# Attention's blocks re-paced over six projection slabs, the gate's operands formed inside the last slab, and a written TensorE order behind it

## The chip, the cores and the metric

The kernel runs on one core of a Trainium2 chip. The metric is the device time of one execution in microseconds (us). TensorE (PE) multiplies, VectorE (DVE), ScalarE (ACT) and GpSimd (POOL) work elementwise, and the queue of SyncE (SP) issues most loads.

## The reference

A trunk of two layers over 512 tokens of width 1024, in float32. Layer 0 is a causal convolution module, layer 1 differential attention with 8 heads; each is followed by a SwiGLU feed-forward part and a gated embedding of the layer's own input `p`. The change touches layer 1's attention, the projection of `p` for its gate, and the product with `w_o`. Cut to that:

```python
u = rms_norm(h, attn_norm_g)
q, k, v = split(u @ w_qkv, 3)             # q, k: 8 heads x 2 halves of 64; v: 8 heads of 128
q = rms_norm(q, q_g) * 64 ** -0.5         # per head and half
k = rms_norm(k, k_g)
for each of 4 blocks of 128 queries, each head, halves c = 0, 1:
    probs[c] = softmax(q[c] @ k[c].T + bias, causal)
    w = probs[0] - lam * probs[1]
    o = w @ v
h = h + (rms_norm(o, sub_g) * (1 - lambda_init)) @ w_o
...                                       # swiglu
h = h + sigmoid(rms_norm(h, ple_g) @ ple_w_gate) * (p @ ple_w_proj)
```

## The kernel before, in words

Every float32 product is done as three products of a reduced format (`mm3`): each operand is split into a high part and a low part. For weights, `weight` loads a 512 KB piece on SP's queue into the ring `wraw` of two buffers (L145), ScalarE casts the high part `whi` (L149), and VectorE, or POOL where `eng=G`, subtracts to get `wlo` (L151). `whi` and `wlo` have four buffers each. A ring buffer is free for the next load when the subtraction that reads it has ended.

The order of instructions on each engine is fixed ahead of time by a scheduler which simulates the program; it follows the order of the code, but lets later instructions go first where an engine would stand idle in its simulation. Each engine then runs its list strictly in that order.

Queries, keys and values are computed in six slabs, in the order of `QKV`: q0, v0, q1, q2, v1, q3. A q slab gives queries and keys of two heads, a v slab the values of four. A slab takes four `weight`s and runs over four blocks of 128 tokens (`tokens`: 8 x 3 products of 128x512 each). For a q slab, each token block ends in `unit` (ScalarE L757, L760; VectorE's sum L764; a root on POOL, L237; POOL's scaling L767) and, a token block later, in `unit_end`: four transposes on TensorE (L773), four evictions on ScalarE (L781, L782), two copies on POOL (L786), and four subtractions on VectorE (L789, L791).

Between a slab's products stand pieces of attention. There are 8 heads x 4 blocks; block (hd, qb) has 128 queries and 128 (qb + 1) keys, and three stages. S: for each half two score products (L818, L819), a biased maximum on VectorE (L821), the exponential on ScalarE (L825), then the weighted difference on VectorE (L828 to L830). T, two blocks later: transposes (L838), split on ScalarE and VectorE (L840, L841). A, three blocks later: products with the values (L854, L855), every second time their sum (L861, L862), and after a head's fourth block the sums for its norm (L866 to L876). `stages` holds all stages in order, each with its block's number n. `pace` tells how much is taken in each token block: 3 x `pace` stages.

Behind the slabs stands the code that the change rewrites. `pfeatures` splits the two operands of `p` (loads L273, ScalarE L274, L275 on VectorE here and on POOL in layer 0) into the tiles C0 and C1; `project` forms eight outputs m, each of six products, from two `weight`s, with a `step` (one stage; when a head is complete, also `stage_o`: transposes L883 and a split by L180 on ScalarE, L181 on VectorE into the A tiles) before each m and after each three products. Then `linear` multiplies with `w_o`: eight outputs of 24 products each; m = 0 and m = 1 run together over k, and the first head whose `ot` is not ready is stepped first.

Of the kernel before, what the change touches and what calls it, by code (L numbers as in the profile page):

```python
# [13 lines left out]
F32R = mybir.dt.float32r  # L14
AF = mybir.ActivationFunctionType
ALU = mybir.AluOpType
# [4 lines left out]
P = 128  # L21
S = 512
D = 1024
NC = D // P
NH = 8
# [49 lines left out]
LA = 3  # L75
# [1 line left out]
PACK = True  # L77
E1 = True
GLO = 1
QKV = (("q", 0, (0, 0, 0, 0)), ("v", 0, (0, 1, 1, 0)), ("q", 1, (1, 1, 2, 2)), ("q", 2, (0, 1, 2, 0)), ("v", 1, (1, 2, 2, 2)), ("q", 3, (0, 2, 0, 1)))  # L80


@with_exitstack
def trunk(ctx, tc, xT, pT, wts, diag, dww, vec, rel, onehot, lamv, out):
    nc = tc.nc
    V, A, G, T = nc.vector, nc.scalar, nc.gpsimd, nc.tensor
# [20 lines left out]
    f = lambda ap: ap.bitcast(F32)  # L107
# [16 lines left out]
    t = wk()[:, 0:P]  # L124
# [4 lines left out]
    t = tp()  # L129
# [4 lines left out]
    wnext = [0]  # L134
    loaded = [None]

    def weight(n=1024, pieces=1, between=(), eng=V, after=(None, None), home=None):
        i = wnext[0]
        wnext[0] += 1
        raw = sb([P, 1024], *(home or ("wraw", 2)))  # L140
        hi = sb([P, 1024], "whi", 4, F32R)
        lo = sb([P, 1024], "wlo", 4, F32R)
        for k in range(pieces):
            cut = slice(k * n // pieces, (k + 1) * n // pieces)
            loaded[0] = nc.sync.dma_start(raw[:, cut], wts[i, :, cut])  # L145
            if k < len(between):
                between[k]()
            with tc.issue_after(after[1].ins) if after[1] else nullcontext():
                A.copy(hi[:, cut], raw[:, cut])  # L149
            with tc.issue_after(after[0].ins) if after[0] else nullcontext():  # L150
                eng.tensor_tensor(lo[:, cut], raw[:, cut], f(hi[:, cut]), ALU.subtract)  # L151
        return hi, lo
# [10 lines left out]
    def both(t):  # L163
        return t[:, 0], t[:, 1]
# [105 lines left out]
    def pfeatures(layer, parts):  # L270
        for k, (hi, lo) in enumerate(parts):
            raw = sb([P, 1024], "wraw", 2)[:, :S]
            nc.sync.dma_start(raw, pT[layer, :, k * S : (k + 1) * S])  # L273
            A.copy(hi, raw)  # L274
            (G if layer == 0 else V).tensor_tensor(lo, raw, f(hi), ALU.subtract)  # L275
        return parts

    last_product = [None]
# [231 lines left out]
    pp = []  # L510
# [67 lines left out]
            if c == 3:  # L578
                third = lo, hi

    def linear(n_in, src, consume, group0=1, before=None, after=None, split={}, home=None):


        m = 0
        while m < NC:
            g = group0 if m == 0 else 1
            ws = [weight(n_in * P, after=split.get(m + i, (None, None)), home=home if m + i == 2 else None) for i in range(g)]
# [290 lines left out]
    ot = {}  # L878
# [15 lines left out]
            if 0 <= at < len(todo):  # L894
                stages.append((n, partial(stage, *todo[at])))

    def take(n):
        got, stages[:n] = [s for _, s in stages[:n]], []
        return got

    waiting = None
    for what, at, pace in QKV:
        ws = slab(GLO if at > 0 else 0)
        for tb in range(4):
            between = take(3 * pace[tb])
# [12 lines left out]

    def step():
        if stages:  # L920
            n, s = stages.pop(0)
            s()
        else:
            n = 99
        while done[0] < NH and (n - LA - 3) // 4 > done[0]:
            stage_o(done[0])
            done[0] += 1

    ph = pfeatures(1, [both(sb([P, 2, S], t, 2, F32R)) for t in ("C0", "C1")])
    pp = []  # L930
    for m in range(NC):
        if m % 4 == 0:
            w = weight()
        step()
        if m < 2:
            o = sb([P, S], f"D{m + 2}", 1)
        elif m % 2 == 0:
            o2 = sb([P, 2, S], f"C{m // 2 + 1}", 2)
            o = o2[:, 0]
        else:  # L940
# [148 lines left out]
```

## Time and profile before

| | |
|---|---|
| Median of 3 runs | 1295.92 us (1295.68 to 1297.31) |
| Profiled execution, time | 1293.82 us |
| Its span on the core | 1292.0 us |
| Mean granted TensorE clock | 0.995 |
| TensorE busy | 1269.5 us (98%) |
| VectorE, ScalarE, POOL busy | 736.9, 521.6, 236.8 us |
| Six slabs | about 640 to 785 us |
| Last of the slabs to the end of `w_o` | 785 to about 881 us |

The profile's page gives each engine's busy time over the span, 40 equal slices of the span, and groups of instructions by line. A row of the timeline has the start, the duration (the modelled end of a matmul overlaps the next), the engine, the line, the tile written and the tiles read, and in brackets the idle time before it with what ended it. A row of waits has the waiting engine and line, then what released it, the total, the number of times, and the longest.

### The profile page before, as it was taken

The numbers are of one execution on the slowest core, as the hardware profiler recorded it, in microseconds if no ns is written. First come the engines' busy times: TensorE is split into PE (matmuls) and PEld (weight loads), VectorE is DVE, ScalarE is ACT, GpSimd is POOL, SyncE is SP. The second block draws the span as 40 slices with busy tenths as digits, with TensorE's granted clock in tenths as the row PEclk, the third lists the DMA queues.
The fourth block names the chain that finished last, engine by engine and source line by source line (L and its number), as shares of the span: only waits on it lengthen the run. The fifth ranks groups of instructions, "written<-read, shape, count | busy, mean of one in ns | idle before, by whom it ended". The sixth has DMA issues, their size and how long they took to land.

```text
span 1292.0 us, 15534 instructions
## 1 busy us (share of the span) xinstructions
PE 1269.5 (98%) x5960; PEld 1053.6 (82%) x5960; DVE 736.9 (57%) x1143; ACT 521.6 (40%) x826; POOL 236.8 (18%) x199
## 2 busy tenths in 40 slices
PE   9999999999999999999999997989999999999998
PEld 8888788888888888888888886878888888888887
DVE  4897866543344334457678988845443344334445
ACT  5742554332222223345566766634222233222332
POOL 1753432000000000042526534121000000000020
PEclk9999999999999999999999998999999999999999
DMA  7555223333333322233222223123333333332231
GB/s 273 192 177 181 80 76 104 98 98 98 98 98 99 97 86 95 82 117 98 88 90 74 74 66 83 57 76 103 99 98 94 89 97 96 98 98 90 90 115 66
DMA packets 46839, 131.98 MB, mean 102 GB/s; under 512 B 5379, under 2 KB 9987, under 8 KB 46764
## 3 DMA queue, kind: packets, MB, share of 16 engines
q1 hardware_dynamic: 44640, 127.55, 31.0%
q10 hardware_dynamic: 2124, 3.43, 1.0%
q8 instruction: 47, 0.77, 0.2%
q14 instruction: 28, 0.23, 0.1%
HBM read 126.75 MB, written 4.21 MB: 101 GB/s over the span
## 4 chain that ended last, share of the span: by engine, by line
PE 88%; DVE 6%; DMA 3%; issue 2%; ACT 1%; POOL 0%; SPq 0%; DVEq 0%; POOLq 0%; ACTq 0%
PE mm L156 28%; PE mm L157 27%; PE mm L158 27%; DVE sc L419 2%; DVE wlo L151 1%; PE tp L173 1%; PE mm L854 1%; DMA wraw<-in_wts 1%; DMA po<-big 1%; PE sc L818 1%; PE sc L368 1%; PE sc L819 1%; PE tp L838 1%; PE tp L773 0%; DMA h<-in_xT 0%
## 5 line engine op out<-in xcount | busy, mean ns | idle before, releaser
L149 ACT CAST whi<-wraw 128x1024 fp32r<-128x1024 f32 (+2 forms) x213 | 217.6, 1026 | 554.6 <-PE mm L158 364.1
L156 PE MATMUL mm<-A,wlo 128*128 128x512 f32 (+1 forms) x1096 | 427.9, 390 | 4.5 <-DVE wlo L151 3.0
L157 PE MATMUL mm<-A,whi 128*128 128x512 f32 (+1 forms) x1096 | 425.7, 389 | 0.0
L158 PE MATMUL mm<-A,whi 128*128 128x512 f32 (+1 forms) x1096 | 421.8, 389 | 0.0
L151 DVE TENSOR_TENSOR wlo<-wraw,whi 128x1024 fp32r<-128x1024 f32 (+2 forms) x209 | 259.4, 1245 | 84.8 <-ACT whi L149 84.7
L156 PEld LDWEIGHTS mm<-A,wlo 128*128 128x128 f32 x1096 | 206.0, 188 | 48.5 <-DVE wlo L151 3.5
L157 PEld LDWEIGHTS mm<-A,whi 128*128 128x128 f32 x1096 | 206.0, 188 | 42.8 <-issue 1.2
L158 PEld LDWEIGHTS mm<-A,whi 128*128 128x128 f32 x1096 | 205.4, 188 | 42.3 <-issue 0.5
L204 POOL TENSOR_TENSOR acc<-acc,wk 128x512 f32<-128x512 f32 x35 | 58.2, 1662 | 772.3 <-issue 660.1
L156 PE MATMUL mm<-B,wlo 128*128 128x512 f32 x352 | 137.8, 391 | 0.0
L157 PE MATMUL mm<-B,whi 128*128 128x512 f32 x352 | 137.4, 390 | 0.0
L158 PE MATMUL mm<-B,whi 128*128 128x512 f32 x352 | 137.4, 390 | 0.0
L635 DVE TENSOR_TENSOR h<-mm,h 128x512 f32<-128x512 f32 x48 | 33.0, 691 | 122.6 <-PE mm L158 122.5
L627 DVE TENSOR_TENSOR big<-mm,rb 128x512 f32<-128x512 f32 x44 | 30.4, 691 | 126.4 <-PE mm L158 126.4
L625 DVE TENSOR_TENSOR big<-mm,rb 128x512 f32<-128x512 f32 x44 | 30.4, 691 | 99.8 <-PE mm L158 93.0
L158 PEld LDWEIGHTS mm<-B,whi 128*128 128x128 f32 x352 | 66.1, 188 | 14.6
L157 PEld LDWEIGHTS mm<-B,whi 128*128 128x128 f32 x352 | 66.1, 188 | 14.3
L156 PEld LDWEIGHTS mm<-B,wlo 128*128 128x128 f32 x352 | 66.0, 188 | 14.2
L156 PE MATMUL mm<-whi,A 128*128 128x512 f32 x192 | 75.9, 396 | 0.0
L157 PE MATMUL mm<-whi,A 128*128 128x512 f32 x192 | 75.5, 393 | 0.0
L158 PE MATMUL mm<-wlo,A 128*128 128x512 f32 x192 | 74.7, 396 | 0.0
L237 POOL TENSOR_TENSOR r<-v,mhalf 128x8 f32<-128x8 f32 (+1 forms) x31 | 45.8, 1477 | 144.3 <-DVE v L235 135.8
(203 smaller groups left out, 1397.4 us busy)
## 6 DMA issues: line engine op xcount, KB each, us to landing
wraw<-in_wts SPq DMA_DIRECT2D x193, 512.0 KB, 3.5
wraw<-in_wts SPq DMA_DIRECT2D x16, 384.0 KB, 3.0
D<-in_diag SPq DMA_DIRECT2D x22, 256.0 KB, 4.3
C<-in_diag SPq DMA_DIRECT2D x16, 256.0 KB, 4.8
h<-in_xT SPq DMA_DIRECT2D x8, 256.0 KB, 5.4
bias<-scr ACTq DMA_DIRECT2D x8, 256.0 KB, 3.5
out_t<-h SPq DMA_DIRECT2D x7, 256.0 KB, 2.0
wraw<-in_wts SPq DMA_DIRECT2D x4, 256.0 KB, 5.0
```

What stands on the lines that cost most here:

```text
L149: A.copy(hi[:, cut], raw[:, cut])
L151: eng.tensor_tensor(lo[:, cut], raw[:, cut], f(hi[:, cut]), ALU.subtract)
L156: T.matmul(acc, al, bh, start=first, stop=False)
L157: T.matmul(acc, ah, bh, start=False, stop=False)
L158: return T.matmul(acc, ah, bl, start=False, stop=last)
L173: r = T.matmul(t[:, cut], src[:, cut], ones, start=first and b == 0, stop=last and b == 3)
L204: self.last = self.eng.tensor_tensor(self.acc, self.acc, sq, ALU.add)
L237: last_pow[0] = G.tensor_tensor(r[:, :n], v[:, :n], mhalf[:, :n], ALU.pow)
L419: last_v_tap[0] = V.scalar_tensor_tensor(sum_, tap(j), wt(c, j), sum_, ALU.mult, ALU.add)
L625: V.tensor_tensor(tg, pg, rb, ALU.mult)
L627: V.tensor_tensor(tu, pu, rb, ALU.mult)
L635: V.tensor_tensor(h[m], acc, h[m], ALU.add)
```

## The change

The pace counts blocks, not stages: `take(n)` advances a count of blocks by n and hands out every stage whose block is below the count, so that T and A come with the S of their own number. Over the slabs 26 blocks are counted; the old table handed out 63 stages, and the new one hands out 73 of 104.

The operands of `p` are formed inside slab q3: `pfeatures` after token block 1, into B0 and B1 (values of the first heads, read for the last time before), with L275 on POOL; the first gate weight after token block 2 into B2 and B3, its L151 on POOL; the second after token block 3 into C0 and C1, its L151 on VectorE. The last `unit_end` moves from the end of the slabs to behind m = 1.

The products of the gate are put under `manual_schedule` for TensorE, which keeps TensorE's instructions there in the order of the code: m = 0 without pieces, then for each m a piece, three products, a piece, three products, a piece, and at most one `stage_o`. The outputs go to C2 to C5 and no longer to D2 and D3.

`w_o`'s weights 4 and 5 get B0, B1 and B2, B3 as their own high and low tiles.

```diff
-QKV = (("q", 0, (0, 0, 0, 0)), ("v", 0, (0, 1, 1, 0)), ("q", 1, (1, 1, 2, 2)), ("q", 2, (0, 1, 2, 0)), ("v", 1, (1, 2, 2, 2)), ("q", 3, (0, 2, 0, 1)))
+QKV = (("q", 0, (0, 0, 0, 0)), ("v", 0, (1, 1, 2, 2)), ("q", 1, (1, 1, 1, 1)), ("q", 2, (1, 1, 2, 2)), ("v", 1, (1, 1, 2, 1)), ("q", 3, (1, 1, 1, 2)))
...
-    def weight(n=1024, pieces=1, between=(), eng=V, after=(None, None), home=None):
+    def weight(n=1024, pieces=1, between=(), eng=V, after=(None, None), home=None, parts=None, bufs=1):
...
-        hi = sb([P, 1024], "whi", 4, F32R)
-        lo = sb([P, 1024], "wlo", 4, F32R)
+        hi = sb([P, 1024], *((parts[0], bufs) if parts else ("whi", 4)), F32R)
+        lo = sb([P, 1024], *((parts[1], bufs) if parts else ("wlo", 4)), F32R)
...
-            (G if layer == 0 else V).tensor_tensor(lo, raw, f(hi), ALU.subtract)
+            G.tensor_tensor(lo, raw, f(hi), ALU.subtract)
...
-    def take(n):
-        got, stages[:n] = [s for _, s in stages[:n]], []
+    taken = [0]
+
+    def take(blocks):
+        taken[0] += blocks
+        got = [s for n, s in stages if n < taken[0]]
+        del stages[: len(got)]
         return got
...
-            between = take(3 * pace[tb])
+            between = take(pace[tb])
...
-    unit_end(*waiting)
+            if (what, at, tb) == ("q", 3, 1):
+                ph = pfeatures(1, [both(sb([P, 2, S], t, 1, F32R)) for t in ("B0", "B1")])
+            elif (what, at, tb) == ("q", 3, 2):
+                pw = [weight(eng=G, parts=("B2", "B3"))]
+            elif (what, at, tb) == ("q", 3, 3):
+                pw.append(weight(parts=("C0", "C1"), bufs=2))
...
-    ph = pfeatures(1, [both(sb([P, 2, S], t, 2, F32R)) for t in ("C0", "C1")])
...
-    for m in range(NC):
-        if m % 4 == 0:
-            w = weight()
-        step()
-        if m < 2:
-            o = sb([P, S], f"D{m + 2}", 1)
-        elif m % 2 == 0:
-            o2 = sb([P, 2, S], f"C{m // 2 + 1}", 2)
-            o = o2[:, 0]
-        else:
-            o = o2[:, 1]
-        pp.append(project(ph, m, w, o, step))
+    with tc.manual_schedule(engines={T.engine}):
+        for m in range(NC):
+            if m % 2 == 0:
+                o2 = sb([P, 2, S], f"C{m // 2 + 2}", 2)
+            if m > 0:
+                piece()
+            pp.append(project(ph, m, pw[m // 4], o2[:, m % 2], piece if m > 0 else lambda: None))
+            if m == 1:
+                unit_end(*waiting)
+            if m > 0:
+                transposed()
...
-    linear(NC, ot, add_attn, 2, heads_until, step)
+    linear(NC, ot, add_attn, 2, heads_until, step, parts={4: ("B0", "B1"), 5: ("B2", "B3")})
```

How the instructions then stand. TensorE behind the last slab's products, where the gate's first product (L156) comes; `sc` is a score, `tp` a transpose, `mm` an accumulator. Before:

```order
L818 MATMUL sc_6637<-C_1154_6147,C_1152_6145 128x384 [waits DVE_49,Pool_49]
L819 MATMUL sc_6637<-C_1156_6149,C_1152_6145 128x384
L773 MATMUL tp_6428<-ident_65,big_6417 128x128 [waits Pool_49]
L773 MATMUL tp_6428<-ident_65,big_6417 128x128 x3
L883 MATMUL tp_6483<-ident_65,D_918_5089 128x128 [waits PE_49]
L883 MATMUL tp_6483<-ident_65,D_918_5089 128x128 x3
L156 MATMUL mm_6520<-C_1210_6443,wlo_6455 128x512 [waits DVE_49]
L157 MATMUL mm_6520<-C_1210_6443,whi_6454 128x512 [waits Activation_49]
```

And now, from the second score of block (6,0) on (B0 and B1 are the operands, B2 and B3 the first gate weight):

```order
L818 MATMUL sc_6449<-C_1165_6183,C_1163_6181 128x128 [waits DVE_49,Pool_49]
L819 MATMUL sc_6449<-C_1167_6185,C_1163_6181 128x128
L854 MATMUL mm_6516<-B_1107_5937,wth_6470 128x256 [waits Activation_49]
L156 MATMUL mm_6564<-B_1200_6350,B_1221_6438 128x512
L157 MATMUL mm_6564<-B_1200_6350,B_1220_6437 128x512
L158 MATMUL mm_6564<-B_1200_6350,B_1220_6437 128x512
L156 MATMUL mm_6564<-B_1201_6351,B_1221_6438 128x512
L157 MATMUL mm_6564<-B_1201_6351,B_1220_6437 128x512
L158 MATMUL mm_6564<-B_1201_6351,B_1220_6437 128x512
L818 MATMUL sc_6487<-C_1164_6182,C_1162_6180 128x256 [waits DVE_49,Pool_49]
L819 MATMUL sc_6487<-C_1166_6184,C_1162_6180 128x256 [waits DVE_49]
L838 MATMUL tp_6504<-ident_65,big_6367 128x128 [waits DVE_49,PE_49]
```

The gate's products of m = 0 now stand ahead of the score of block (6,1), and behind an L854 that waits for ScalarE's L840.

ScalarE around the same place, before (the first L149 is the gate's first weight):

```order
L840 CAST wth_6383<-tp_6381 128x128
L274 CAST C_1211_6444<-wraw_6449 128x512
L781 ACTIVATE C_1152_6145<-tp_6399,lam_4521 64x2x128
L782 ACTIVATE C_1154_6147<-tp_6399,vec_63 64x2x128
L781 ACTIVATE C_1153_6146<-tp_6399,lam_4521 64x2x128
L782 ACTIVATE C_1155_6148<-tp_6399,vec_63 64x2x128
L825 ACTIVATE big_6527,st_6201<-big_6527,st_6201 128x512
L866 ACTIVATE wk_6469<-D_1174_6234 128x512
L825 ACTIVATE rb_6533,st_6201<-rb_6533,st_6201 128x512
L692 DMA bias_6739<-scr 128x512
L825 ACTIVATE big_6564,st_6560<-big_6564,st_6560 128x128
L149 CAST whi_6454<-wraw_6453 128x1024
```

And now (C_1246 is the second gate weight, each `whi` one of `w_o`'s weights 1 and 2; L840 is the one that the L854 above waits for):

```order
L149 CAST C_1246_6556<-wraw_6555 128x1024
L149 CAST whi_6934<-wraw_6933 128x1024
L781 ACTIVATE C_1162_6180<-tp_6407,lam_4521 64x2x128
L782 ACTIVATE C_1164_6182<-tp_6407,vec_63 64x2x128
L781 ACTIVATE C_1163_6181<-tp_6407,lam_4521 64x2x128
L782 ACTIVATE C_1165_6183<-tp_6407,vec_63 64x2x128
L840 CAST wth_6470<-tp_6466 128x384
L861 COPY D_1231_6481<-mm_6392 128x256
L825 ACTIVATE big_6452,st_6448<-big_6452,st_6448 128x128
L825 ACTIVATE acc_6457,st_6448<-acc_6457,st_6448 128x128
L149 CAST whi_7054<-wraw_7053 128x1024
L286 COPY C_1248_6563<-mm_6564 128x512
```

The weights' casts now stand ahead of a unit end's evictions L781 and L782, of L840, and of the exponentials L825.

TensorE in the slabs, the longest piece there without one of a slab's own products. Before (14 rows in all, 12 of them here):

```order
L773 MATMUL tp_5810<-ident_65,big_5723 128x128 [waits DVE_49,PE_49,Pool_49]
L773 MATMUL tp_5810<-ident_65,big_5723 128x128 x3
L838 MATMUL tp_5863<-ident_65,big_5629 128x128 [waits DVE_49]
L855 MATMUL mm_5835<-B_855_4824,wtl_5795 128x128
L854 MATMUL mm_5835<-B_869_4898,wth_5794 128x256
L855 MATMUL mm_5835<-B_869_4898,wtl_5795 128x128
L854 MATMUL mm_5835<-B_881_4954,wth_5794 128x256
L855 MATMUL mm_5835<-B_881_4954,wtl_5795 128x128
L854 MATMUL mm_5835<-B_883_4982,wth_5794 128x256
L855 MATMUL mm_5835<-B_883_4982,wtl_5795 128x128
L818 MATMUL sc_5905<-C_899_5012,C_897_5010 128x512 [waits DVE_49]
L819 MATMUL sc_5905<-C_901_5014,C_897_5010 128x512
```

Now, in slab q2 (30 rows in all, 12 of them here):

```order
L818 MATMUL sc_5541<-C_916_5077,C_914_5075 128x512 [waits Pool_49]
L819 MATMUL sc_5541<-C_918_5079,C_914_5075 128x512
L818 MATMUL sc_5614<-C_915_5076,C_913_5074 128x128 [waits DVE_49]
L819 MATMUL sc_5614<-C_917_5078,C_913_5074 128x128
L773 MATMUL tp_5578<-ident_65,big_5520 128x128 [waits PE_49,Pool_49]
L773 MATMUL tp_5578<-ident_65,big_5520 128x128 x3
L838 MATMUL tp_5631<-ident_65,big_5442 128x128 [waits PE_49]
L838 MATMUL tp_5631<-ident_65,big_5442 128x128 x2
L818 MATMUL sc_5652<-C_915_5076,C_913_5074 128x256 [waits DVE_49]
L819 MATMUL sc_5652<-C_917_5078,C_913_5074 128x256
L818 MATMUL sc_5614<-C_916_5077,C_914_5075 128x128 [waits DVE_49]
L819 MATMUL sc_5614<-C_918_5079,C_914_5075 128x128
```

Scores of several blocks now follow each other, each waiting for VectorE.

TensorE in `w_o`, from the last of the products of m = 0 to 3 on to m = 4. Before:

```order
L158 MATMUL mm_6864<-A_1362_7015,whi_6853 128x512 [waits DVE_49]
L158 MATMUL mm_6865<-A_1362_7015,whi_6859 128x512
L158 MATMUL mm_7057<-A_1362_7015,whi_7052 128x512
L158 MATMUL mm_7096<-A_1362_7015,whi_7091 128x512
L156 MATMUL mm_7135<-A_1223_6488,wlo_7131 128x512 [waits DVE_49]
L157 MATMUL mm_7135<-A_1223_6488,whi_7130 128x512 [waits Activation_49]
```

And now:

```order
L158 MATMUL mm_6939<-A_1361_6996,whi_6928 128x512 [waits DVE_49]
L158 MATMUL mm_6940<-A_1361_6996,whi_6934 128x512
L158 MATMUL mm_7059<-A_1361_6996,whi_7054 128x512
L158 MATMUL mm_7098<-A_1361_6996,whi_7093 128x512
L156 MATMUL mm_7137<-A_1265_6645,B_1384_7133 128x512 [waits DVE_49]
L157 MATMUL mm_7137<-A_1265_6645,B_1383_7132 128x512
```

The low and high part of weight 4 are now B tiles, and the wait for the cast (Activation) is gone. The three products of m = 3 that stood ahead of the last four L883 stand partly behind them.

More of the change, by code (lines that the diff above doesn't have):

```diff
@@ L579, in trunk, with linear @@
                 third = lo, hi
-    def linear(n_in, src, consume, group0=1, before=None, after=None, split={}, home=None):
+    def linear(n_in, src, consume, group0=1, before=None, after=None, split={}, home=None, parts={}):
         m = 0
@@ L586, in linear @@
             g = group0 if m == 0 else 1
-            ws = [weight(n_in * P, after=split.get(m + i, (None, None)), home=home if m + i == 2 else None) for i in range(g)]
+            ws = [weight(n_in * P, after=split.get(m + i, (None, None)), home=home if m + i == 2 else None, parts=parts.get(m + i)) for i in range(g)]
             accs = [mm() for _ in range(g)]
@@ L913, in trunk, with transposed, piece, step @@
                 waiting = unit(at, ws, tb, between)
-    unit_end(*waiting)
-    done = [0]
[L919 to L922, printed above, removed]
-        else:
-            n = 99
-        while done[0] < NH and (n - LA - 3) // 4 > done[0]:
+            if (what, at, tb) == ("q", 3, 1):
[4 more added lines that the diff above has]
+                pw.append(weight(parts=("C0", "C1"), bufs=2))
+    done = [0]
+    def transposed():
+        if done[0] < NH and (now[0] - LA - 3) // 4 > done[0]:
             stage_o(done[0])
             done[0] += 1
-    ph = pfeatures(1, [both(sb([P, 2, S], t, 2, F32R)) for t in ("C0", "C1")])
-    pp = []
-    for m in range(NC):
-        if m % 4 == 0:
-            w = weight()
-        step()
-        if m < 2:
-            o = sb([P, S], f"D{m + 2}", 1)
-        elif m % 2 == 0:
-            o2 = sb([P, 2, S], f"C{m // 2 + 1}", 2)
-            o = o2[:, 0]
-        else:
-            o = o2[:, 1]
-        pp.append(project(ph, m, w, o, step))
+    now = [0]
+    def piece():
+        now[0], s = stages.pop(0) if stages else (99, lambda: None)
+        s()
+    def step():
+        piece()
+        transposed()
+    pp = []
+    with tc.manual_schedule(engines={T.engine}):
[3 more added lines that the diff above has]
+            if m > 0:
+                piece()
+            pp.append(project(ph, m, pw[m // 4], o2[:, m % 2], piece if m > 0 else lambda: None))
+            if m == 1:
+                unit_end(*waiting)
+            if m > 0:
+                transposed()
     def heads_until(k):
```

## The prediction, as put on record before the changed kernel had run

> **What bounds the kernel now.** I read the page's busy shares first, then the windows of the attention's end, the waits of TensorE there, and TensorE's own rows where they name an idle time.
>
> ```profile
> PE 1269.5 (98%) x5960; PEld 1053.6 (82%) x5960; DVE 736.9 (57%) x1143; ACT 521.6 (40%) x826; POOL 236.8 (18%) x199
> ```
>
> TensorE is the bound: 1269.5 of 1292.0 us, so all its idle time is 22 us. A change that leaves the arithmetic alone can win only there, and where the clock is low. In windows (time, then PE, PEld, DVE, ACT and POOL busy, then the granted clock):
>
> ```profile
> 640.00:785.00 145.00, 142.95 (x752) 120.99 (x751) 119.57 (x311) 97.39 (x228) 67.96 (x69) 1.00 0.22 72
> 790.00:800.00 10.00, 4.39 (x15) 3.60 (x16) 7.81 (x24) 5.92 (x14) 4.66 (x5) 0.60 0.57 134
> 800.00:810.00 10.00, 8.13 (x38) 6.09 (x37) 9.62 (x25) 8.10 (x18) 1.91 (x3) 0.89 0.63 193
> 850.00:860.00 10.00, 6.19 (x28) 4.61 (x27) 6.53 (x7) 4.77 (x7) 2.58 (x2) 1.00 0.09 15
> 785.35:827.02 41.67, 32.91 (x176) 27.31 (x175) 37.69 (x109) 33.30 (x79) 9.05 (x10) 0.88 0.35 96
> ```
>
> So the six slabs (640 to 785) lose 2.05 us, the stretch behind them 785.35 to 810 some 8.7, and W_o's middle (850 to 860) 3.8. The waits there:
>
> ```profile
> PE sc L818 <- DVE st L821: 5.7, 6, 1.4
> PE mm L156 <- DVE wlo L151: 4.7, 2, 3.0
> PE sc L818 <- DVE v L871: 2.7, 1, 2.7
> PE mm L156 <- ACT A L180: 0.8, 1, 0.8
> ```
>
> And where they lie, from the slab's last matmul to the last score product and on into W_o:
>
> ```profile
> 784.89 0.39 PE L157 MATMUL mm<-whi,A 128*128 128x512 f32 x1
> 785.12 0.39 PE L158 MATMUL mm<-wlo,A 128*128 128x512 f32 x1
> ...
> 791.20 0.33 PE L818 MATMUL sc<-C,C 128*128 128x128 f32 x1 [1.31 <-DVE st L821]
> 794.35 0.66 PE L818 MATMUL sc<-C,C 128*128 128x384 f32 x1 [2.71 <-DVE v L871]
> ...
> 798.74 0.80 PE L156 MATMUL mm<-C,wlo 128*128 128x512 f32 x1 [1.70 <-DVE wlo L151]
> 799.33 0.63 PE L157 MATMUL mm<-C,whi 128*128 128x512 f32 x1
> 799.76 0.63 PE L158 MATMUL mm<-C,whi 128*128 128x512 f32 x1
> ...
> 826.79 0.39 PE L819 MATMUL sc<-C,C 128*128 128x512 f32 x1
> 851.86 0.50 PE L156 MATMUL mm<-A,wlo 128*128 128x512 f32 x1 [0.78 <-ACT A L180]
> 857.90 0.50 PE L156 MATMUL mm<-A,wlo 128*128 128x512 f32 x1 [3.03 <-DVE wlo L151]
> ```
>
> A 512-column product costs 0.23 us at the full clock (784.89 to 785.12) and 0.43 at the low one (799.33 to 799.76). Some 5.2 us were busy at the low clock between 794.35 and 802; nearly half of it, 2.1, is loss. All that can be won from 640 to 860 is 2.05 + 8.7 + 2.1 + 3.8 = 16.7 us.
>
> Two things end the wait at 798.74: the gate's weight comes late, and VectorE is full.
>
> ```profile
> 790.24 0.69 DVE L275 TENSOR_TENSOR C<-wraw,C 128x512 fp32r<-128x512 f32 x1
> 796.38 1.04 ACT L149 CAST whi<-wraw 128x1024 fp32r<-128x1024 f32 x1 [4.03 <-DMA wraw<-in_wts]
> 797.45 1.23 DVE L151 TENSOR_TENSOR wlo<-wraw,whi 128x1024 fp32r<-128x1024 f32 x1 [2.05 <-ACT whi L149]
> ```
>
> The two ring buffers are held by the operands until L275 ends, so the weight lands at 796.38. But VectorE is busy 37.69 of the 41.67 us up to the last score (last row of the windows); it, not the weight alone, paces this end.
>
> **The change, part by part.**
>
> *Operands and weights inside slab q3.* Loads, casts and subtractions of the gate go ahead of the slab's end, and the wait at 798.74 (1.70, and 4.03 on ScalarE) goes. On SP's queue the gate's four loads and W_o's first two now stand in the slab; W_o's second load waits for the first one's subtraction and lands by my walk some 5 us after the first transposes of q3. On ScalarE the casts of W_o and of the second gate weight now stand ahead of the unit ends of token blocks 0 and 1 (L781, L782, 0.47 each), so a late load there holds four evictions, then L840, then L854 on TensorE, which in the written order has matmuls behind it. I walk that as a stall of 3 us before the gate's first product, 5 before the score of block (6,2) and 2 before (6,3): 10 us, as much idle as now, but over a shorter stretch.
>
> *Subtractions moved to POOL.* L275 twice and one L151 leave VectorE, 2 x 0.78 + 1.23 = 2.8 us. But POOL's subtraction is not free for VectorE:
>
> ```profile
> 687.93 2.41 POOL L151 TENSOR_TENSOR wlo<-wraw,whi 128x1024 fp32r<-128x1024 f32 x1 [2.20 <-ACT whi L149]
> 688.02 2.73 DVE L830 SCALAR_TENSOR_TENSOR big<-acc,st,big 128x384 f32<-128x384 f32 x1
> ...
> 748.77 2.40 POOL L151 TENSOR_TENSOR wlo<-wraw,whi 128x1024 fp32r<-128x1024 f32 x1 [2.30 <-ACT whi L149]
> 749.37 1.81 DVE L829 SCALAR_TENSOR_TENSOR st<-st,lam 128x1 f32<-128x1 f32 x1
> ...
> 754.00 0.41 PE L818 MATMUL sc<-C,C 128*128 128x384 f32 x1 [1.38 <-DVE st L821]
> ```
>
> ```profile
> L829 DVE SCALAR_TENSOR_TENSOR st<-st,lam 128x1 f32<-128x1 f32 x8 | 1.7, 213 | 0.0
> L830 DVE SCALAR_TENSOR_TENSOR big<-acc,st,big 128x384 f32<-128x384 f32 x2 | 1.2, 617 | 0.0
> L275 POOL TENSOR_TENSOR wtl<-wraw,wtl 128x512 fp32r<-128x512 f32 x1 | 1.3, 1291 | 1.1 <-ACT wtl L274 1.1
> ```
>
> Both times VectorE's instruction ended when POOL's did: 2.73 for 0.62, 1.81 for 0.21, so 1.6 to 2.1 us lost of each 2.4, and TensorE waited 1.38 soon after the second. The Trainium skill, "GPSIMD Engine Reference", section "Key points", says that GpSimd shares its SBUF interfaces with VectorE and contends with VectorE instructions of two SBUF inputs; these rows agree, and by it the move saves VectorE nothing. By the rows, 2.4 + 2 x 1.29 us on POOL cost VectorE between 0 (nothing with two inputs meets them) and 4.1, against the 2.8 saved. I take a net of zero.
>
> *New pace in the slabs.* Ahead of the slab's end go 2.0 us of TensorE work (by the order: two score halves, three L838, five L854/L855 pairs, less one unit end), and on VectorE, of the 37.69 us, four L151 (4.9), two L275 (1.6) and some 7 us of attention. The slabs pay: in q2, thirty attention instructions now stand without a matmul between them, with eight scores; between its scores of (.,512) and (.,384) VectorE has some 4.1 us to do against 2.3 on TensorE, and about 2 us of waiting for L789/L791 stand ahead of it. Two lesser bunches take about 1 each. Against them the 2.05 us lost now fall partly away. What a slab asks of VectorE follows from groups like these:
>
> ```profile
> L821 DVE CUSTOM_DVE_ANT_0 big<-sc,bias 128x512 f32<-128x512 f32 x3 | 2.1, 685 | 0.0
> L821 DVE CUSTOM_DVE_ANT_0 big<-sc,bias 128x128 f32<-128x128 f32 x2 | 0.6, 280 | 0.0
> L841 DVE TENSOR_TENSOR wtl<-tp,wth 128x512 fp32r<-128x512 f32 x2 | 1.4, 676 | 0.0
> L791 DVE SCALAR_TENSOR_TENSOR C<-tp,vec,C 64x256 fp32r<-64x256 f32 x4 | 1.9, 484 | 0.1
> L764 DVE TENSOR_REDUCE v<-wk 128x8 f32<-128x512 f32 x1 | 0.7, 686 | 0.1
> ```
>
> A block is two L821, an L830 and an L841 (by its width 1.2 to 2.8 us together), the small L828 and L829, and its share of its head's L862, L868 to L874 and L181: 3.3 us over four widths. The slab's own is 15 us: three L151 (3.7) and four times a sum, its root and two pairs L789/L791 (2.8). TensorE has 96 x 0.23 = 22 us of slab, 1.4 of unit ends and 1.3 a block. With six blocks that is 34.8 on VectorE against 31.2 on TensorE, the balance to be made up by neighbours with less. Net +3; ends 0 (VectorE was busy 119.57 of 145, so there is room) and +7 (3.6 of that balance in q2, and the bunches).
>
> *The end, up to the last score.* Now 41.67 us behind the slab's end. VectorE's list there shrinks by 13.5 to 24.2 us; at today's share of busy time (0.904) that makes 27. From the first eviction of q3 on, though, its list shrinks by only 6.7, which makes 35, since it comes to the slab's end with work left over; the walk of the waits gives 36 (33 to 39). I take 33.5, nearer to the last two: -8.2. To be given back: the 2.0 moved into the slabs, and 3.1 of TensorE work which stood ahead of the last score and now stands behind it (36 products there for 56, 20 x 0.23 = 4.6, less 1.5 of attention). Net -3.1; ends -9.6 at 27 and +2.4 at 39.
>
> *W_o.* Weights 4 and 5 have buffers of their own, so their casts don't wait for weights 0 to 3; 3.03 goes. Three products now stand between the last L883 and the row that waits for L180, so most of the 0.78 goes. What hides the new casts is the rest of the gate and 22 us of W_o. I take -3.5, ends -3.8 and -2.5.
>
> *The outputs in C instead of D* cost nothing: same instructions.
>
> Sum: +3 - 3.1 - 3.5 = -3.6 from 1293.82 us, the profiled execution: 1290.2. The median of the runs, 1295.92, lies 2.1 above that execution, so the forecast for a median is 1292.3.
>
> **Rivals.** (1) Slower: q2 runs at VectorE's rate. The balance of 3.6 is paid in full, its bunch takes another 4, a POOL hold inside it 2, and VectorE enters q3 late, so that the last score comes at 39 (+2.4): +12 - 3.5 = +8.5 at worst, about +4 likely, 1300. It decides once the slabs lose over 9 us. For it: the 1.38 at 754.00 behind one POOL hold; against it: 25 us of VectorE's time free before 785. (2) Nothing won in the end: ScalarE, behind casts that wait for loads, holds L781 to L840, and the written order lets no matmul pass, so the 8.7 us only change place; W_o's 3.5 pays the slabs' 3: 1295.5. For it: the 4.03 before L149 above. Against: the loads start in the slab. (3) The low clock comes back. In 790 to 800, 5.6 us idle gave 0.60; in 850 to 860 a 3.03 us gap left 1.00. A stall of 5 us in the new end would bring the 2.1 us again, 1294.4. The Trainium skill, "TensorE: Matmul & The Clock Gate", section "Part 1: The HAM clock gate", puts the switch at an idle window of about 3.4 us: both rows agree. (4) All of it goes: 12 to 14 of the 16.7, 1282 to 1284; against it VectorE's 0.904.
>
> **Numbers.** 0.2% (2.6 us) is about what a measurement of this kernel tells from no change. Forecast 0.45 and (4) 0.07: faster 0.52. (2) 0.15 and (3) 0.10: within, 0.25. (1): 0.23. The best of the ends is -3.8 - 9.6 + 0 = -13.4, the worst +7 + 2.4 - 2.5 = +6.9; leaving a tenth off each side, 1285.5 to 1299.5; the forecast's own range is 1287 to 1293.3.
>
> **What will show it.** Right: no row of 3 us at the gate's first product; the last L819 33.5 us behind the slab's last matmul; no 3.03 in W_o; clock 1.00 throughout; 4 to 6 us idle in the slabs, most in q2. Wrong: L818 waits of over 9 us in the slabs (1); a long wait on ScalarE at L149 with L773 and L818 behind it (2); a window under 0.9 (3). If VectorE's instructions meet POOL's subtractions in q3 with 2 us each, the end is later than 33.5. I should be wrong above all if VectorE keeps up in q2, or if the walked 10 us of stalls are not there.

## The result and the profile after

The changed kernel takes 1311.14 us (median of 4 runs, 1309.59 to 1313.06) against 1296.62 for the kernel before on the same chip: a ratio of 1.0113, 95% interval 1.0095 to 1.0130. It is slower by some 14.7 us, where 1292.3 had been forecast.

TensorE is as full as before, over a longer span (page of the changed kernel):

```profile
span 1311.3 us, 15537 instructions
PE 1279.3 (98%) x5960; PEld 1058.3 (81%) x5960; DVE 735.7 (56%) x1140; ACT 524.2 (40%) x826; POOL 247.2 (19%) x202
```

Its work is the same 5960 TensorE instructions, so the 9.8 us more of busy time are instructions at a lower clock and, as I take it, small waits that the modelled ends hide. Windows of the changed kernel, from the first eviction of q0 to the slabs' end, three pieces of that, and the end up to the last score:

```profile
631.41:807.74 176.33, 165.13 (x818) 136.49 (x817) 132.00 (x335) 111.43 (x248) 82.77 (x75) 0.97 0.24 78
690.00:700.00 10.00, 8.05 (x42) 6.53 (x40) 3.96 (x5) 4.63 (x8) 9.09 (x7) 1.00 0.14 31
720.00:730.00 10.00, 7.39 (x33) 5.55 (x32) 7.44 (x21) 5.68 (x14) 5.11 (x6) 0.85 0.00 0
730.00:740.00 10.00, 8.25 (x34) 6.59 (x33) 8.20 (x28) 7.99 (x19) 6.73 (x6) 0.81 0.12 29
807.74:846.55 38.81, 28.39 (x156) 23.80 (x155) 33.68 (x94) 29.11 (x70) 11.90 (x12) 0.87 0.22 71
```

Cut at the same places, the two profiled executions compare so (us; "rest" runs from the last score to VectorE's first product of the feed-forward part):

| | slabs | end, to the last score | rest | sum |
|---|---|---|---|---|
| before | 156.5 | 41.4 | 71.3 | 269.2 |
| changed | 176.3 | 38.8 | 70.8 | 286.0 |
| difference | +19.9 | -2.6 | -0.5 | +16.8 |

Another 2.5 us stood ahead of the first eviction already, in layer 0, which the change leaves alone; the medians, which lie closer together than these two executions, carry no more than 14.7. So the whole loss lies in the slabs. TensorE's waits there, in the changed kernel:

```profile
PE mm L854 <- ACT wth L840: 8.4, 7, 2.0
PE sc L818 <- DVE st L821: 1.2, 4, 0.5
PE sc L818 <- POOL C L786: 0.6, 1, 0.6
PE tp L838 <- DVE big L830: 0.4, 1, 0.4
PE mm L855 <- DVE wtl L841: 0.4, 1, 0.4
```

These 11.0 us stand against 2.1 before: 8.9 more. The clock takes 4.8 us away (TensorE's busy time in each stretch of 2 us, times the share that the granted clock lacks there; before: none). With the 2.0 us of work moved in, that makes 15.7 of 19.9; the rest are, as I take it, small waits without a row of their own. VectorE's busy time is not what bounds the slabs: it is busy 132.0 of 176.3 us, a smaller share than before (126.1 of 156.5).

The longest of the seven waits for L840, TensorE, then ScalarE, of the changed kernel:

```profile
697.05 0.60 PE L773 MATMUL tp<-ident,big 128*128 128x128 f32 x4
697.48 0.49 PE L838 MATMUL tp<-ident,big 128*128 128x128 f32 x3
699.92 0.39 PE L854 MATMUL mm<-B,wth 128*128 128x256 f32 x1 [1.95 <-ACT wth L840]
```

```profile
697.68 0.47 ACT L781 ACTIVATE C<-tp,lam 64x256 fp32r<-64x256 f32 x1 [2.33 <-PE tp L773]
698.05 0.46 ACT L782 ACTIVATE C<-tp,vec 64x256 fp32r<-64x256 f32 x1
698.54 0.47 ACT L781 ACTIVATE C<-tp,lam 64x256 fp32r<-64x256 f32 x1
698.91 0.46 ACT L782 ACTIVATE C<-tp,vec 64x256 fp32r<-64x256 f32 x1
699.39 0.48 ACT L840 CAST wth<-tp 128x384 fp32r<-128x384 f32 x1
```

A unit end's transposes, a block's transposes and that block's value products stand in one row without a slab product between them. ScalarE takes four evictions first, then L840; TensorE waits 1.95 us. In six of the seven (7.8 of the 8.4 us) a unit end's four evictions stand ahead of that L840 on ScalarE, twice with exponentials among them; on TensorE, slab products or scores stand in between in the other five of these. Just ahead of the wait shown, for some 12 us, TensorE had run nearly nothing but slab products, and VectorE had starved (3.96 of 10 us busy from 690 to 700). POOL was the busy one then (9.09 us), but no unit end's transpose waits for it in the rows above. The scheduler had bunched the two kinds of work.

### The profile page after: what moved, and what is told of

It is laid out like the page before. It is cut to its first block, busy times and chain, and to the rows that moved or that the text cites. A ratio compares the mean times of both kernels' runs of the same rounds, so it can differ in the third digit from the quotient of the medians.

```text
span 1311.3 us, 15537 instructions
## 1 busy us (share of the span) xinstructions
PE 1279.3 (98%) x5960; PEld 1058.3 (81%) x5960; DVE 735.7 (56%) x1140; ACT 524.2 (40%) x826; POOL 247.2 (19%) x202
## 4 chain that ended last, share of the span: by engine, by line
PE 82%; DVE 7%; DMA 3%; ACT 3%; issue 3%; POOL 2%; SPq 0%; ACTq 0%; DVEq 0%; POOLq 0%
PE mm L156 26%; PE mm L157 26%; PE mm L158 26%; DVE sc L419 2%; DVE wlo L151 2%; POOL wk L407 1%; DMA wraw<-in_wts 1%; PE mm L854 1%; DMA po<-big 1%; ACT whi L149 1%; PE sc L818 1%; ACT C L781 0%; ACT C L782 0%; PE sc L819 0%; DMA h<-in_xT 0%
## 5 line engine op out<-in xcount | busy, mean ns | idle before, releaser
L149 ACT CAST whi<-wraw 128x1024 fp32r<-128x1024 f32 (+2 forms) x209 | 214.0, 1028 | 552.2 <-PE mm L158 355.5
L156 PE MATMUL mm<-A,wlo 128*128 128x512 f32 (+1 forms) x1080 | 421.6, 390 | 1.1 <-ACT A L180 1.0
L157 PE MATMUL mm<-A,whi 128*128 128x512 f32 (+1 forms) x1080 | 419.5, 389 | 0.0
L158 PE MATMUL mm<-A,whi 128*128 128x512 f32 (+1 forms) x1080 | 415.5, 389 | 0.0
L151 DVE TENSOR_TENSOR wlo<-wraw,whi 128x1024 fp32r<-128x1024 f32 (+2 forms) x205 | 254.9, 1247 | 85.6 <-ACT whi L149 85.2
L156 PEld LDWEIGHTS mm<-A,wlo 128*128 128x128 f32 x1080 | 202.9, 188 | 44.0 <-ACT A L180 1.9
L157 PEld LDWEIGHTS mm<-A,whi 128*128 128x128 f32 x1080 | 203.0, 188 | 42.2 <-issue 1.2
L158 PEld LDWEIGHTS mm<-A,whi 128*128 128x128 f32 x1080 | 202.6, 188 | 41.6 <-issue 0.5
L156 PE MATMUL mm<-B,wlo 128*128 128x512 f32 x352 | 137.8, 391 | 0.0
L158 PEld LDWEIGHTS mm<-B,whi 128*128 128x128 f32 x352 | 66.1, 188 | 14.5
L156 PEld LDWEIGHTS mm<-B,wlo 128*128 128x128 f32 x352 | 66.1, 188 | 14.2
L156 PE MATMUL mm<-whi,A 128*128 128x512 f32 x192 | 76.9, 400 | 0.0
L237 POOL TENSOR_TENSOR r<-v,mhalf 128x8 f32<-128x8 f32 (+1 forms) x31 | 48.4, 1560 | 117.5 <-DVE v L235 114.2
```

The lines of the kernel that those rows point to most:

```text
L156: T.matmul(acc, al, bh, start=first, stop=False)
L157: T.matmul(acc, ah, bh, start=False, stop=False)
L158: return T.matmul(acc, ah, bl, start=False, stop=last)
L237: last_pow[0] = G.tensor_tensor(r[:, :n], v[:, :n], mhalf[:, :n], ALU.pow)
```

## The experiments

All are judged by the ratio to the kernel before on the same chip, three rounds each. "A" in their texts is the theory that the new table is the loss, "B" that the rest of the change is. Edits that appear in several are shown once.

**Which part costs.** The old pace in the changed kernel:

```diff
-            between = take(pace[tb])
+            between = take(3 * pace[tb])      # old table, old take()
```

> The changed kernel with the old pace of the slabs (three stages for each unit of the old table); all else as changed. Theory A, the new pace is the loss: the slabs fall back from 176.3 us to about 158 and the rest keeps its gains at the end and in W_o, so 1290 to 1296 us, at or below before. Theory B, the operands formed in the last slab and the written order are the loss: it stays at 1306 to 1311.

Measured: 1298.43 us, ratio 1.0010 (0.9998 to 1.0023). The slabs are back at 156.5 us. Only the new pace in the kernel before:

> The kernel before with only the new pace (blocks counted, new table). Theory A: the slabs lose as in the changed kernel, some 18 us net of the work moved into them, and the end behind them wins nothing or a little: 1308 to 1316 us. Theory B: within 3 us of before, 1294 to 1300.

Measured: 1321.42 us, 1.0183 (1.0167 to 1.0200), slabs 174.5; slower still than theory A had it. Theory A holds: the table alone costs 24 us, and taking it away gives 13 back. But the rest of the change is worth nothing with the old table, where I had expected a gain; so it was taken apart too. W_o's homes alone:

> The kernel before with only the homes of W_o's weights 4 and 5 in B0 to B3. Both theories: the 3.03 us ahead of m = 4 go and nothing else moves, so 2.5 to 3.5 us below before, about 1293.5. A rival: the gap only moves to weight 6 or 7 behind it, no change.

Measured: 1294.73 us, 0.9977 (0.9968 to 0.9987), 3.0 us less, as expected. The wait of 3.03 us ahead of m = 4 is gone.

**The end's parts.** With the old pace, the three subtractions back on VectorE, then the written order away:

```diff
-            G.tensor_tensor(lo, raw, f(hi), ALU.subtract)
+            (G if layer == 0 else V).tensor_tensor(lo, raw, f(hi), ALU.subtract)
...
-                pw = [weight(eng=G, parts=("B2", "B3"))]
+                pw = [weight(parts=("B2", "B3"))]
```

> The changed kernel with the old pace, and the gate's three moved subtractions (twice L275, once L151) on VectorE as before and not on POOL. If POOL's two-input subtractions stop VectorE, as in the slabs before, the move had won nothing: within 1 us of the run with the old pace (1298.4), or up to 2 us less. If VectorE's relief was worth its 2.8 us, it is 2 to 3 us more: 1300 to 1301.

Measured: 1297.10, 1.0006 (0.9994 to 1.0017): no difference that can be told from the old-pace run.

```diff
-    with tc.manual_schedule(engines={T.engine}):
+    with nullcontext():
```

> The changed kernel with the old pace and without the written order of TensorE behind the slabs (the scheduler sets it, as before the change). If the written order holds matmuls back behind transposes that wait for VectorE (4.4 and 3.3 us of such waits in the run with the old pace), the end gets shorter by 3 to 6 us: 1292.5 to 1295.5. If VectorE's list is what sets the end whatever TensorE's order, within 1.5 us of 1298.4.

Measured: 1293.41, 0.9975 (0.9963 to 0.9988): the written order costs some 4.5 us. The waits behind the slabs, first of the old pace with it, then without:

```profile
PE tp L773 <- DVE C L791: 4.4, 2, 3.1
PE tp L838 <- DVE wtl L841: 3.2, 2, 3.1
PE sc L818 <- DVE st L821: 3.0, 3, 2.1
```

```profile
PE tp L773 <- DVE C L791: 2.8, 2, 1.7
PE sc L818 <- DVE st L821: 2.4, 2, 1.7
```

With the written order, transposes that wait for VectorE hold the gate's products behind them; the scheduler lets these go first. With the new table:

> The changed kernel, new table, without the written order behind the slabs. With the old table taking that order away was worth 5 us; if the order costs whatever the table, 1304 to 1308. If the written order is what keeps the end of the new table short (the table alone cost 24 us and the whole change 14.5), it gets slower, 1312 to 1318. The slabs stay within 1 us of 176.3 in both.

Measured: 1308.28, 1.0103 (1.0083 to 1.0123), slabs 173.8, 2.5 us less and not the same. The interval meets the changed kernel's (1.0095 to 1.0130), so a cost of the order is not shown there, a gain from it neither. Both edits on the old pace:

> The old pace, no written order, the three subtractions on VectorE: what is left of the change is the operands formed in the last slab and W_o's homes. If POOL's subtractions cost some 1.3 us as with the written order (1298.4 to 1297.1), 1292 to 1293; if they relieve VectorE, 1294 to 1295. Beside it the run with W_o's homes alone stood at 1294.7.

Measured: 1289.55 us, 0.9954 (0.9938 to 0.9971). That is below the range expected. It beats both kernels, and what it keeps is mainly the operands formed in the last slab and W_o's homes. Its waits behind the slabs:

```profile
PE sc L818 <- DVE st L821: 3.0, 3, 2.2
PE mm L156 <- ACT A L180: 0.8, 1, 0.8
PE sc L818 <- DVE v L872: 0.6, 1, 0.6
```

The wait of the gate's first product (1.70 before) is gone. So, step by step as ratios to before: W_o's homes 0.9977; with the operands in the slab, on VectorE, 0.9954; with their subtractions on POOL 0.9975; with the written order 1.0010; with the new table 1.0113. The intervals of the first three overlap from step to step; the written order and the table stand clear.

**Why the table costs.** The other tables, blocks counted in v0, q1, q2, v1, q3 (the changed kernel: 1122 1111 1122 1121 1112, 26 blocks):

| run | counts | written order behind the slabs | slabs, us | us | ratio |
|---|---|---|---|---|---|
| light | 0111 1111 1111 1112 1112 | yes | 158.6 | 1306.92 | 1.0072 |
| v0 light | 0111 1111 1122 1121 1112 | yes | 162.9 | 1317.51 | 1.0153 |
| no twos | 1122 1111 1111 1111 1112 | yes | 167.3 | 1316.33 | 1.0150 |
| q1 late | 1122 1100 1122 1121 1112 | yes | 161.8 | 1308.04 | 1.0092 |
| late | 0112 1111 0121 1222 1201 | no, DVE | 166.9 | 1305.85 | 1.0059 |
| early | 0112 1221 1100 1222 1201 | no, DVE | 163.2 | 1305.21 | 1.0054 |
| q1 late | 1122 1100 1122 1121 1112 | no, DVE | 161.7 | 1300.37 | 1.0017 |

> The changed kernel with a lighter table, 21 blocks and not 26: none in the first token block behind q0, then one in each, two in the last of v1 and of q3. Theory A1, slabs with six blocks overfill VectorE: the slab loss falls from 18 to 5 us or less, 1295 to 1299 in all. Theory A2, any table with a block in nearly every token block makes attention's sums take the accumulators in turn with the slabs, so that the token blocks run one by one and nothing fills attention's waits: 1304 or more.

Light: the slabs are only 2.2 us longer than before, as A1 has it, but the whole is as A2 has it: the blocks left over make the end longer (56.0 us for 41.4).

> The changed kernel with three blocks in slab v0 for six (0,1,1,1); the other slabs' counts as changed, 23 blocks in all. Theory A1a, the six blocks in v0 put VectorE behind and the later slabs inherit the delay: the slabs take 160 to 164 us for 176.3, and the whole 1298 to 1302. Theory A3, the twos in q2 and v1 are what TensorE pays for: the slabs stay above 168 us, 1304 or more.

V0 light: the slabs came to 162.9, as A1a said; the whole did not: the end took 63.1 us for 38.8, with 19.0 us of TensorE idle, 9.1 of them one L773 that waits for POOL's L767 of the last unit in the written order. No twos has the same wait with 9.8 us, and q1 late with the written order has it with 9.1.

> The changed kernel with v0 as changed (1,1,2,2) and no two in q2 and v1 (one block in each token block), 23 blocks in all. Theory A1a: the slabs stay above 168 us, 1306 or more. Theory A3: they fall to 160 to 164, 1298 to 1302.

No twos: the slabs, 167.3, met neither range. To q2's last eviction it takes 115.8 us, the changed kernel 114.7, though 26 more slab products, some 6 us, already stand in that stretch. TensorE's idle time and lost clock (as above) up to there are 11.4 us for 12.7: the twos in q2 cost little, and A3 falls as the main cause.

An accumulator (a PSUM bank) for attention's sums, three for the rest:

```diff
-            oacc[hd, qb // 2] = mm()
+            oacc[hd, qb // 2] = mm(True)     # a bank of its own; slabs and gate rotate over three
```

> The changed kernel, new table, with the four accumulators parted in the attention: three for the slabs' and the gate's products, one for attention's sums. Theory A2, the token blocks wait for accumulators that attention's sums hold, so TensorE has no matmul to fill attention's waits with: the slabs fall from 176.3 us to 165 or less. Theories A1a (VectorE behind) and A4 (attention has caught up with the queries) see no change or a loss: 174 or more.

Measured: 1309.72, 1.0106 (1.0091 to 1.0121). The slabs fell to 163.1, as A2 asked. To q2's last eviction they took 117.0, no less, but that mark misleads: 368 slab products stand ahead of it for 320 in the changed kernel, 48 of v1's let forward, some 11 us at 0.23 each. Idle time and lost clock in the slabs fell from 16.0 us to 6.3, and no wait for L840's copy is left there. But the end grew from 38.8 to 48.5 us, its idle time and lost clock from 14.0 to 21.4, and the whole is where it was. So the banks are not ruled out: with the same table, parting them changes the scheduler's order so that the loss leaves the slabs and comes back behind them.

> The changed kernel with slab q1's counts (1,1,0,0) for (1,1,1,1), all other counts as changed, so that the first two blocks of head 2, whose queries and keys are made in q1 itself, are taken in q2. Theory A4, a block taken a token block or two behind the making of its own queries puts the whole round of transposes, evictions and subtractions on TensorE's path: from the first eviction of q0 to q2's last one 114.7 us fall to about 102, the slabs to 162 or less. Theory A1a, the six blocks in v0 are the load that delays everything: 111 or more to q2's last eviction, the slabs above 170.

q1 late: to q2's last eviction 101.2 us (expected: about 102), slabs 161.8, as A4 has it. Head 2's queries come from q1; putting off its four blocks, each taken one token block after their own making, was worth 13.5 us up to there, 2.6 of it the work of the two blocks put off (1.3 each). Yet the whole fell by some 3 us only, 1308.04 (1.0077 to 1.0107, which meets the changed kernel's interval), for the end grew from 38.8 to 53.7 us. Idle time and lost clock went from 16.0 to 6.1 us in the slabs and from 14.0 to 21.0 behind them, the same picture as with the parted banks. And is it the earliness, or the load with it? The next two differ in the earliness alone.

> Blocks counted, no written order, the three subtractions on VectorE; counts v0 (0,1,1,2), q1 (1,1,1,1), q2 (0,1,2,1), v1 (1,2,2,2), q3 (1,2,0,1): head 2's four blocks are taken from the second token block of q2 on. Both theories: slabs of 156 to 161 us; the whole 1289 to 1295.

> As the late one, but q1 (1,2,2,1) and q2 (1,1,0,0): the same counts up to v0 and from q2's end on, and head 2's blocks each taken one token block behind the making of their queries. If taking them early is the cause: the slabs take 165 us or more and the whole is 5 us or more above the late one. If the load in v0 is: within 2 us of the late one.

The late one met neither of its numbers, which both theories had set: slabs 166.9, 1305.85 in all. Early and late come out alike (1.0054, 1.0037 to 1.0072, and 1.0059, 1.0042 to 1.0076). To q2's last eviction early costs 3.4 us (100.6 for 97.2), some 2 of them nine more slab products, and the late one loses that again in v1. So with four blocks in v0 earliness isn't dear; in the changed kernel it stands together with six.

> The changed kernel's table with q1 (1,1,0,0), no written order, the three subtractions on VectorE: 24 blocks against the 21 to 23 of the old pace. If more blocks in the slabs shorten the end by what they cost there, 1289 to 1292, level with the best run so far (1289.6); if the six blocks in v0 still cost some 4 us in the slabs (161.8 against 156.5), 1293 to 1297.

q1 late without the written order: 1300.37 us, above both ranges: no table that I tried comes near the old one (1289.55 with the same rest).

What goes along with the slabs' length is the longest row of attention instructions that the scheduler made without a slab product in it. Counted in the rows of the traces (somewhat fewer than in the order's listing) it is 13 in the old table (no loss) and in the light one (+2.2 us against 156.5), 18 early (+6.7), 19 in both q1-late ones (+5.3, +5.2) and with the banks parted (+6.6), 21 in no twos and late (+10.8, +10.4), 22 in v0 light (+6.4), 26 in the changed kernel (+19.9), in the table alone (+18.0) and in the table without written order (+17.3). The last two runs took these rows away by writing TensorE's order in the slabs too (a piece after each three products):

```diff
+    with tc.manual_schedule(engines={T.engine}):
     for what, at, pace in QKV:
...
-            between += [None] * (6 - len(between))
+            between += [None] * (7 - len(between))
```

> The changed kernel's new table without the written order behind the slabs, but with TensorE's order written in the slabs: a piece of attention after each three products, and the unit end a token block later as the last piece. No row of more than 8 attention instructions is left there. If the scheduler's bunches are what the new table costs: slabs of 158 to 166 us against 173.8 in the run with the new table and no written order, waits of L854 for L840 under 3 us, and 1292 to 1300 in all. If attention cannot keep up in itself: the waits only change their names, 172 or more in the slabs. A rival on the way: the unit ends' transposes (L773) wait for POOL's scaling in this order, one to two us in each of 16.

> The same written order in the slabs with the old pace, on the best kernel so far (no written order behind the slabs, subtractions on VectorE). If bunches are what costs, there is little to win, its rows being 14 at most: 156 to 159 us in the slabs, 1288 to 1293 in all. If the unit ends wait in this order, 160 or more in the slabs.

Measured: 1342.93 (1.0352) with the new table, 1336.17 (1.0301) with the old; slabs 221.8 and 206.8, some 8 us of each for 35 products of q0 that in the other runs stand ahead of the first eviction. The expectation failed: the waits of L854 for L840 are all but gone, but others take their place, and in the order of the code TensorE waits more than in the bunches (34 and 29 us idle in the slabs, 11 in the changed kernel). So the bunches are the scheduler's lesser evil, and what a bunch costs by itself is not shown. But the two runs show where the new table waits when the scheduler moves nothing about; the one with the old table has the three subtractions on VectorE besides. Waits from 630 to 860 us, the new table first, then the old:

```profile
PE sc L818 <- DVE st L821: 17.7, 14, 4.2
PE sc L818 <- DVE C L789: 10.7, 4, 4.0
PE tp L773 <- POOL big L767: 4.9, 3, 3.1
```

```profile
PE sc L818 <- DVE st L821: 17.8, 14, 5.6
PE mm L158 <- DVE wlo L151: 5.1, 5, 2.3
PE tp L773 <- POOL big L767: 3.5, 2, 3.3
```

The 10.7 us are four scores, and their shapes and the table name them, head 2's blocks of 128 to 512 keys, each waiting for a subtraction of its own unit end:

```profile
699.37 0.30 PE L818 MATMUL sc<-C,C 128*128 128x128 f32 x1 [1.78 <-DVE C L789]
712.50 0.35 PE L818 MATMUL sc<-C,C 128*128 128x256 f32 x1 [2.45 <-DVE C L789]
727.62 0.42 PE L818 MATMUL sc<-C,C 128*128 128x384 f32 x1 [3.97 <-DVE C L789]
740.40 0.47 PE L818 MATMUL sc<-C,C 128*128 128x512 f32 x1 [2.47 <-DVE C L789]
```

So it is shown that the table is the loss, and that taking the twos out leaves most of it in the slabs (12.2 of 16.0 us idle or at a low clock). Two edits, either of them alone, take most of the slabs' loss away: putting head 2's blocks off gives back 14.5 of 19.9 us (2.6 of them work put off), parting the banks 13.2 with the table kept. With the written order behind the slabs, the end takes nearly all of it back; without that order putting the blocks off keeps more (1.0017 against 1.0103), though that run has the subtractions on VectorE besides. Which property of the table makes the slabs dear, early blocks or accumulators held, is not settled. It also stays open why the tables without early blocks still lose: they leave TensorE 4.8 to 10.0 us idle or at a low clock in the slabs, the old one 2.1, and the scheduler's order changes as a whole with each table.

## Why the prediction was wrong, point by point

**The pace in the slabs: +3 with ends 0 and +7; measured +17.9** (19.9 less the 2.0 of moved work). This is the step that failed. I had priced it by VectorE's balance in q2 and by VectorE's work between the scores of one bunch. In the runs VectorE had time to spare, and a lighter q2 did little. The price that the rows show is in latency: value products that wait for L840 behind a unit end's four evictions on ScalarE, six times, 7.8 of the 8.9 us by which the waits grew; and in the clock (4.8 us), which I had forecast at 1.00. The bunch that I had read off the order (30 rows, eight scores) was there, but it is only one of the places. Why the new table brings these waits out stays open.

**Rivals.** (1) had the sign, about 1300 (+8.5 at worst) and "once the slabs lose over 9 us", with a chance of 0.23. Its mechanism, q2 at VectorE's rate, was not the one. (2), with 0.15, came true as far as the end goes: TensorE idles 10.4 us there up to the last score, 8.7 before. (3), with 0.10, came true beside it: there was a stall of 4.9 us, and the granted clock of that stretch is 0.87, before 0.88. The lost clock there was mis-sized too: 3.2 us before by windows of 2 us, where the sum has 2.1.

**The end: 33.5 us to the last score; measured 38.8.** The walk of the waits had said 36 (33 to 39) and stalls of 3, 5 and 2 us. They came nearly as walked:

```profile
810.34 0.30 PE L818 MATMUL sc<-C,C 128*128 128x128 f32 x1 [1.08 <-DVE v L235]
811.92 0.39 PE L854 MATMUL mm<-B,wth 128*128 128x256 f32 x1 [1.18 <-ACT wth L840]
822.09 0.69 PE L818 MATMUL sc<-C,C 128*128 128x384 f32 x1 [4.90 <-POOL C L786]
830.01 0.47 PE L818 MATMUL sc<-C,C 128*128 128x512 f32 x1 [1.94 <-DVE C L789]
```

2.3 (the first two rows, ahead of the gate's first product), 4.9 and 1.9 us; the 4.9 ended on POOL's copies. To blend the walk with VectorE's busy share was the mistake: that share set nothing here, where the chain of waits was longer. End and rest together won 3.1 us, where -3.1 and -3.5 and the 2.0 that moved had made 8.6.

**W_o: -3.5; measured -3.0** alone (interval 1.7 to 4.1). Right.

**Subtractions on POOL: net 0.** On the best kernel the ratio went from 0.9954 to 0.9975 with them, some 2.7 us, but the intervals just overlap: a cost is likely and not shown. In the written order nothing could be told. The rows show the hold (POOL, then VectorE, of the changed kernel):

```profile
776.42 2.40 POOL L151 TENSOR_TENSOR wlo<-wraw,whi 128x1024 fp32r<-128x1024 f32 x1 [7.78 <-ACT whi L149]
776.69 2.15 DVE L871 TENSOR_TENSOR v<-v,r 128x4 f32<-128x4 f32 x1
795.82 2.40 POOL L151 TENSOR_TENSOR B<-wraw,B 128x1024 fp32r<-128x1024 f32 x1 [0.27 <-ACT B L149]
797.02 1.21 DVE L871 TENSOR_TENSOR v<-v,r 128x4 f32<-128x4 f32 x1
```

An instruction of 0.15 us lasts until POOL is done. The second pair is the gate's weight, moved to POOL by this change: 1.1 us lost of the 1.23 saved. The Trainium skill, "GPSIMD Engine Reference", section "Key points" (the interfaces shared with VectorE), is borne out.

**The clock.** The Trainium skill, "TensorE: Matmul & The Clock Gate", section "Part 1: The HAM clock gate", speaks of an idle window of some 3.4 us. Here the longest wait in the slabs is 1.95 us, and the clock still fell. Windows of the changed kernel:

```profile
722.00:724.00 2.00, 1.16 (x10) 0.92 (x8) 1.25 (x5) 1.94 (x6) 0.35 (x1) 1.00 0.00 0
724.00:726.00 2.00, 0.59 (x2) 0.39 (x3) 1.56 (x4) 1.95 (x6) 1.88 (x3) 1.00 0.00 0
726.00:728.00 2.00, 1.65 (x6) 1.21 (x6) 1.90 (x6) 0.80 (x3) 1.24 (x2) 0.73 0.00 0
728.00:730.00 2.00, 2.00 (x8) 1.36 (x8) 2.00 (x6) 1.00 (x3) 0.00 (x0) 0.50 0.00 0
```

Two gaps, 1.61 and 0.64 us, leave TensorE busy 1.75 of 4 us, and the next stretch runs at half. By that window alone the clock would have stayed at 1.00; the measurement decides. In the prediction I had let two rows agree with it, but from 790 to 800 the longest gap was 2.71 us, and the clock was at 0.50 from 792 on, before that gap had ended. A low busy share does not settle it either: the kernel before was busy 0.97 of the 4 us from 854 to 858 and kept 1.00. What sets the clock's fall stays open.

## What to carry to other kernels

Before a table feeds more work into a busy engine, ask of each piece how many engines in a row it has to pass, and what stands ahead of it on each, not only how busy those engines are: here four evictions ahead of one cast cost 7.8 us in six places that no busy share showed. The walk of the waits was the better forecast of the end than a busy share (36 us against 27, for 38.8). Judge a stage together with what stands behind it: two edits took 13 and 14.5 us out of the slabs, and the whole hardly moved. And take a bundled change apart before judging it: here two of its parts won 6 us together, and three others lost 20.

## What the runs showed of the hardware

Holding goes both ways between POOL and VectorE. POOL's root L237 (128x8) took 1.64 us twelve times; the other four times, 2.47 to 2.62 us, VectorE's 128x1024 subtraction ran beside it for 0.98 us or more (in one of the twelve for 0.79). One of these four held up POOL's copies, with which the 4.9 us wait above ended (VectorE, then POOL, of the changed kernel):

```profile
818.87 1.22 DVE L151 TENSOR_TENSOR wlo<-wraw,whi 128x1024 fp32r<-128x1024 f32 x1
819.04 2.54 POOL L237 TENSOR_TENSOR r<-v,mhalf 128x8 f32<-128x8 f32 x1 [4.10 <-DVE v L235]
821.65 0.85 POOL L786 CAST C<-C 64x256 fp32r<-64x256 f32 x2
```
